# A decoder block on one core: the second group's first weights a step later, small loads behind x's tiles, x2's stores ahead of gate's rows

## The chip, the cores and the metric

The kernel runs on one core of one Trainium2 chip. The metric is device time in microseconds (us) of one execution, lower is better. The kernel before takes 1216.88 us, the median of three runs (1215.8 to 1218.68). All numbers of the profile come from one further execution, taken by the hardware profiler.

## What is computed

One layer for 1024 tokens of width 1024, all in float32. The reference, cut to what matters:

```python
h = rms_norm(x, norm1_g)
rq, rk, rv, rg, dq, dk, dv = split(h @ w_in)            # 512 columns each
# eight retention heads: rotary on q and k, chunks of 128 tokens with a running state
ret = rms_norm(retention(rotary(rq), rotary(rk) * 64 ** -0.5, rv), ret_norm_g) * silu(rg)
# four differential heads: two softmax maps each over normed q and k
q_d, k_d = rms_norm(dq, diff_q_norm_g), rms_norm(dk, diff_k_norm_g)
lam = exp(sum(lambda_q1 * lambda_k1)) - exp(sum(lambda_q2 * lambda_k2)) + LAMBDA_INIT
dif = (softmax(q1 k1^T / 8) - lam * softmax(q2 k2^T / 8)) @ dv
dif = rms_norm(dif, diff_subln_g) * (1 - LAMBDA_INIT)
x = x + concat([ret, dif]) @ w_out
h2 = rms_norm(x, norm2_g)
x = x + (silu(h2 @ w_gate) * (h2 @ w_up)) @ w_down      # 2816 hidden columns
```

## The kernel before

**Split products.** A float32 operand is held as two parts: `hi`, rounded by ScalarE (ACT), and `lo`, the rest, taken by VectorE (DVE). Each product is three matmuls on TensorE (PE): hi by hi, hi by lo, lo by hi. Weights come in rows of 128 (a tile `raw`), are scaled and split by `load_w` into `whi` and `wlo`, and stay in SBUF for a group. In the profile, a split of a weight is one ACT row `whi<-raw` and one DVE row `wlo<-raw`. There are two `raw` buffers, so a third row is not loaded before the first has been split.

**Steps.** Steps 0 to 31 are the four differential heads by eight token tiles. In step s the projection of head s // 8 and tile s % 8 (`proj`, 8 chunks of three matmuls, 384 wide, into a PSUM tile `pp`) is the spine; after each chunk k stand the pieces of other work that `DIF_PLAN` names as (lag, k, function). So the attention of a tile runs one to three steps behind its projection: `d_sq` and `d_qkn` norm q and k, `d_qkturn` turns them (PE, `m<-cs,qkn`), `d_qkhi`, `d_qlo`, `d_klo` split them into `q`, `kh`, `kl`, `d_scores` multiplies (`big<-kh,q`), `d_max`, `d_exp`, `d_weights` make the softmax. Beside this, x itself is turned in steps 0 to 5: `x_load(t)` brings tile t (SyncE's queue, tile `p`), `x_turn(t, half)` turns it (PE, `m<-cs,p`, four 128x128), `x_split(t, half)` splits the turned half (ACT `CAST act<-m`, then DVE `act<-m,act`). Tiles 0 to 3 are loaded at the start, tile t from 4 on in step t - 3, and turned in step t - 2. All turns share two PSUM buffers `m`: a turn waits until what was turned two turns back has been split.

**Weights of the next group.** The table `ready` gives each step the rows of weights that are loaded for it (`w_load(s + 1)`, at the beginning of step s) and split in it (`w_part(s)`, ACT behind chunk 5 and DVE behind chunk 6). Head 1's row k stands at step k: one row a step from step 0 on.

**Small loads.** `small_loads` at the end of step 0 issues ten little transfers: the gains `gq`, `gk` (two each), the four lambda vectors (`lam`) and the two output gains (`gout`). In step 1 `gains` scales gq and gout, and `lambdas` makes minus lambda (`nlam`): product and sum on DVE (`lprod`, `lsum`), `lexp` on ACT, two rows on DVE.

**After the heads.** Steps 32 to 63 are retention (512 wide), steps 64 to 66 the first three tiles of the output projection. `r_tables` makes retention's tables `rms`, `vdec`, `eps` on DVE from the means `ms`. Then `mid` runs the remaining 13 half tiles of the output projection, 8 chunks each, with `MID_PLAN` naming (chunk, function): `o_load` loads a half tile of x (`xr`), `o_add` adds it to the product and stores the sum to DRAM (`x2d<-x`), `n_square`, `n_rs`, `n_scale` norm it in place (so `n_scale` waits for the store), `n_turn` turns it (PE, `h<-cs,x`). Gate's first two blocks of weights (`rawp<-in_w_gate_dram`, 512 KB each) are asked for at chunks 40 and 56, up's at chunk 111. The rest, from about 594 us on, is the feed-forward: `Strassen` products of seven matmul groups, one pair of gate and up columns at a time, then w_down.

**What sets the order.** Every engine takes its instructions in order. While `order["pinned"]` is set, the instructions that go through the wrapper `Pinned` stand as written; all else is placed by a scheduler, as early as its data and buffers allow. Before the change the wrapper covers the four computing engines, not SyncE (SP), and `r_tables` is called with pinning off. SP's queue issues nearly all transfers, one after the other; an issue that has to wait holds those behind it. The wrapper's line 377 stands in the profile as the source of every computing instruction, so rows are told apart by tile names.

Of the kernel before, what the change touches and what calls it, by code (L numbers as in the profile page):

```python
# [16 lines left out]
P = 128  # L17
# [3 lines left out]
KC = D // P  # L21
# [31 lines left out]
def constants():  # L53
# [68 lines left out]
    (0, "mix_turn", 0),  # L122
    (0, "o_load", 0, 1),
    (0, "mix_turn", 1),
# [239 lines left out]
def block_kernel(ctx: ExitStack, tc: tile.TileContext, x, norm1_g, w_in, ret_norm_g, dq_g, dk_g,  # L364
# [16 lines left out]

    V, A, G, T = Pinned(nc.vector), Pinned(nc.scalar), Pinned(nc.gpsimd), Pinned(nc.tensor)

    const = ctx.enter_context(tc.tile_pool(name="const", bufs=1))
# [149 lines left out]
    def load_x(t):  # L534
        xt[t] = dp.tile([P, S], F32, tag="p", name="p", bufs=NP)
        nc.sync.dma_start(xt[t], x[0, t * P:(t + 1) * P, :])

# [77 lines left out]
    def small_loads():  # L615
        for g_sb, g_dr in ((gq, dq_g), (gk, dk_g)):
            for m in range(2):
                nc.sync.dma_start(g_sb[m * HD:(m + 1) * HD, :], g_dr[0].rearrange("(d o) -> d o", o=1))
        for i, l_dr in enumerate((lq1, lq2, lk1, lk2)):
            nc.sync.dma_start(lam4[:, i, :], l_dr[0].partition_broadcast(P))  # L620
        nc.sync.dma_start(gout[:, 0:4], ret_norm_g[0].rearrange("h d -> (h d)").rearrange("(k p) -> p k", p=P))
        nc.sync.dma_start(gout[:, 4:5], subln_g[0].rearrange("(d o) -> d o", o=1))
# [4 lines left out]
    def gains():  # L627
        V.tensor_scalar_mul(gq, gq, HD ** -0.5)
        V.tensor_scalar_mul(gout[:, 0:4], gout[:, 0:4], HD ** 0.5)
        V.tensor_scalar_mul(gout[:, 4:5], gout[:, 4:5], 1.0 - LAMBDA_INIT)  # L630

    def lambdas():
        lprod = dp.tile([P, 2, HD], F32, tag="sqo", name="lprod", bufs=1)
        V.tensor_tensor(out=lprod, in0=lam4[:, 0:2, :], in1=lam4[:, 2:4, :], op=ALU.mult)
        V.tensor_reduce(out=lsum, in_=lprod, axis=AX.X, op=ALU.add)
        A.activation(lexp, lsum, AF.Exp)
        V.tensor_tensor(out=nlam, in0=lexp[:, 1:2], in1=lexp[:, 0:1], op=ALU.subtract)
        V.tensor_scalar_add(nlam, nlam, -LAMBDA_INIT)
# [305 lines left out]
    def o_add(t, dh):  # L944
        x2[t][dh] = (rowa if dh else rowb).tile([P, 512], F32, tag="rowa" if dh else "rowb", name="x2")
        V.tensor_tensor(out=x2[t][dh], in0=prs.pop(("o", t, dh)), in1=prs.pop(("x", t, dh)), op=ALU.add)
        nc.sync.dma_start(x2d[t * P:(t + 1) * P, dh * 512:(dh + 1) * 512], x2[t][dh])

# [6 lines left out]
    for g in range(1, NG + 1):  # L955
        for k in range(KC):
            s = (g - 1) * NT + k
            if g == NDH + 1:
                s = max(s, (g - 1) * NT + 4 + k // 2)
            ready.setdefault(s, []).append((g, k, "wp" if g % 2 == 0 else "wd" if g < NDH else "wr"))  # L960
# [17 lines left out]
    for s in range(ND + NR + 3):  # L978
        if s == ND:
# [6 lines left out]
            for qbd in qbd_t:  # L986
                G.memset(qbd, 0.0)
            r_tables()
        if s == ND + 2:
            difps.close()  # L990
# [11 lines left out]
        elif s == 1:  # L1002
            ops += [(5, gains), (7, lambdas)]
            ops += [(at, f, 2, *args) for at, f, *args in LATE]
        ops += [(0, w_load, s + 1)] + [(k, w_part, s) for k in W_PLAN]
        t = s - ND - NR
# [128 lines left out]
    class Strassen:  # L1135
# [9 lines left out]
        def load(self, j):  # L1145
            r = ap.tile([P, 4, 2, P], F32, tag="rawp", name="rawp", bufs=3)
            nc.sync.dma_start(r.rearrange("p k i e -> p k (i e)"),
                              self.source[0, j * 512:(j + 1) * 512, self.f0 * P:(self.f0 + 2) * P].rearrange(
# [251 lines left out]
```

## Time and profile before

| | |
|---|---|
| time, median of 3 runs | 1216.88 us (1215.8 to 1218.68) |
| time of the profiled execution | 1216.8 us |
| its span from first to last instruction | 1215.0 us |
| PE busy | 1200.5 us (99%), 5968 matmuls |
| DVE, ACT, POOL busy | 835.5, 537.1, 556.1 us |
| mean granted PE clock | 0.998 |

The span is 1.8 us shorter than the time of the same execution. PE's busy time counts a matmul from its start to its modelled end; successive matmuls overlap, so what counts for the path is where a row says that PE stood idle and for whom. The granted clock is the share of full speed that PE was given in a stretch: a matmul takes longer while it is below 1.

### The profile page before, as it was taken

The page shows a single profiled execution, that of the slowest core. Times are in us where ns is not written, and L with a number is a line of the kernel's source. Part 1 is how long each engine was busy: PE and PEld are TensorE (multiplying, and loading weights), DVE is VectorE, ACT ScalarE, POOL GpSimd, SP SyncE. Part 2 cuts the span into 40 slices and gives each one's busy share as a digit, 9 for nine tenths or more (in the row PEclk, how much of TensorE's full clock was granted, in tenths as well). Part 3 has the DMA queues.
Part 4 walks back from the last instruction along what each step waited for, and adds up shares of the span by engine and source line. Part 5 has one row for each costly group of instructions (what it writes and reads, how often), then busy time and mean ns, then how long its engine had stood idle before and what let it go on. Part 6 is the DMA issues. An engine that isn't in the chain of part 4 may idle for free.

```text
span 1215.0 us, 17362 instructions
## 1 busy us (share of the span) xinstructions
PE 1200.5 (99%) x5968; PEld 1020.6 (84%) x5968; DVE 835.5 (69%) x1501; ACT 537.1 (44%) x1194; POOL 556.1 (46%) x709
## 2 busy tenths in 40 slices
PE   7999999999999999999999999999999999999998
PEld 6899989888888888788888888888888888888887
DVE  5988888864444445545989766766666659798697
ACT  5866666653322233433634344343443434444442
POOL 2655555545444434100056556544565436154053
PEclk9999999999999999999999999999999999999999
DMA  6201011103111111422133333323333168943342
GB/s 202 62 27 32 22 36 36 36 10 102 46 36 44 35 35 36 148 92 91 61 104 122 113 104 113 115 85 104 105 113 114 68 233 289 365 136 95 95 120 81
DMA packets 97383, 117.34 MB, mean 97 GB/s; under 512 B 8976, under 2 KB 60304, under 8 KB 97296
## 3 DMA queue, kind: packets, MB, share of 16 engines
q1 hardware_dynamic: 95968, 115.65, 29.5%
q8 instruction: 47, 0.77, 0.3%
q10 hardware_dynamic: 1328, 0.60, 0.2%
q14 instruction: 40, 0.33, 0.1%
HBM read 87.64 MB, written 28.57 MB: 96 GB/s over the span
## 4 chain that ended last, share of the span: by engine, by line
PE 94%; DVE 3%; DMA 1%; ACT 1%; issue 1%; POOL 0%; DVEq 0%; ACTq 0%; POOLq 0%
PE pp L377 43%; PE h L377 27%; PE m L377 19%; PE big L377 3%; PE o L377 2%; PE it L377 1%; DMA raw<-in_w_in_dram 1%; DVE act L377 1%; DMA x2d<-x 0%; DVE wlo L377 0%; DVE q L377 0%; DVE x L377 0%; DVE acc L377 0%; ACT kh L377 0%; DVE sum L377 0%
## 5 line engine op out<-in xcount | busy, mean ns | idle before, releaser
L377 PE MATMUL pp<-whi,act 128*128 128x384 f32 (+1 forms) x896 | 287.2, 373 | 0.8 <-ACT whi L377 0.8
L377 POOL TENSOR_TENSOR sum<-rawp 128x512 f32<-128x512 f32 x100 | 142.0, 1422 | 174.0 <-DVE wlo L377 172.3
L377 ACT CAST whi<-sum 128x512 fp32r<-128x512 f32 x165 | 102.6, 622 | 201.8 <-POOL sum L377 65.7
L377 DVE TENSOR_TENSOR wlo<-sum,whi 128x512 fp32r<-128x512 f32 x165 | 166.4, 1008 | 35.0 <-ACT whi L377 34.8
L377 PE MATMUL h<-act,whi 128*128 128x512 f32 x608 | 187.2, 389 | 0.0
L377 PEld LDWEIGHTS pp<-whi,act 128*128 128x128 f32 x896 | 167.2, 189 | 15.3 <-ACT whi L377 1.0
L377 PE MATMUL pp<-wlo,act 128*128 128x384 f32 (+1 forms) x448 | 161.6, 361 | 0.6 <-DVE wlo L377 0.6
L377 POOL TENSOR_TENSOR sum<-wide 128x512 f32<-128x512 f32 x55 | 86.9, 1581 | 127.4 <-DVE wlo L377 99.0
L377 PEld LDWEIGHTS h<-act,whi 128*128 128x128 f32 x608 | 114.1, 188 | 23.6
L377 PE MATMUL pp<-wrh,act 128*128 128x512 f32 x384 | 131.3, 402 | 0.0
L377 PE MATMUL h<-act,wlo 128*128 128x512 f32 x304 | 118.3, 389 | 0.0
L377 DVE TENSOR_TENSOR wlo<-wide,whi 128x512 fp32r<-128x512 f32 x99 | 79.2, 823 | 32.1 <-ACT whi L377 32.1
L377 PE MATMUL pp<-act,whi 128*128 128x512 f32 (+2 forms) x320 | 97.2, 385 | 0.2 <-DVE act L377 0.2
L377 PE MATMUL m<-act,whi 128*128 128x512 f32 (+2 forms) x320 | 97.0, 385 | 0.0
L377 ACT CAST whi<-wide 128x512 fp32r<-128x512 f32 x99 | 59.3, 621 | 83.4 <-PE m L377 43.2
L377 PEld LDWEIGHTS pp<-wlo,act 128*128 128x128 f32 x448 | 84.9, 190 | 7.7 <-DVE wlo L377 1.2
L377 PEld LDWEIGHTS pp<-wrh,act 128*128 128x128 f32 x384 | 72.2, 188 | 14.3
L377 POOL TENSOR_TENSOR fsum<-c 128x512 f32<-128x512 f32 x55 | 79.3, 1452 | 10.0 <-DMA ffd<-fsum 10.0
L377 DVE TENSOR_TENSOR c<-c,h 128x512 f32<-128x512 f32 x86 | 56.8, 682 | 30.0 <-PE h L377 30.0
L377 PE MATMUL pp<-wrl,act 128*128 128x512 f32 x192 | 74.8, 390 | 0.0
L377 DVE TENSOR_TENSOR wlo<-rawp,whi 128x512 fp32r<-128x512 f32 x44 | 47.8, 1087 | 38.7 <-ACT whi L377 37.9
L377 PEld LDWEIGHTS pp<-act,whi 128*128 128x128 f32 x320 | 59.8, 188 | 12.2 <-DVE act L377 0.4
(163 smaller groups left out, 2514.8 us busy)
## 6 DMA issues: line engine op xcount, KB each, us to landing
wide<-ffd SPq DMA_DIRECT2D x77, 256.0 KB, 2.8
ffd<-fsum SPq DMA_DIRECT2D x55, 256.0 KB, 2.0
rawp<-in_w_gate_dram SPq DMA_DIRECT2D x22, 512.0 KB, 3.8
rawp<-in_w_up_dram SPq DMA_DIRECT2D x22, 512.0 KB, 3.8
wide<-in_w_down_dram SPq DMA_DIRECT2D x44, 256.0 KB, 5.4
raw<-in_w_in_dram SPq DMA_DIRECT2D x32, 256.0 KB, 2.8
ffd<-c SPq DMA_DIRECT2D x22, 256.0 KB, 2.0
raw<-in_w_in_dram SPq DMA_DIRECT2D x26, 192.0 KB, 2.5
```

The costliest lines, as they stand in the source:

```text
L377: i = getattr(self.engine, op)(*args, **kw)
```

## The change

- Head 1's row 0 moves from step 0 to step 1, where row 1 already stands: two rows are split in step 1, none in step 0. In step 1 the loads for step 2 (`w_load`) stand behind the last chunk in place of the first.
- Of the ten small loads, `gq` and `gk` stay; the four of lambda and the two of `gout` become `late_loads` in step 1. The scaling of `gout` and lambda's product and sum move to step 2 (chunk 2), its exponential and the two rows behind it to chunk 6 of step 2.
- SP gets a wrapper of its own, `SY`, which is used for x's tiles, x2's stores and gate's and up's blocks: these now stand in program order among the pinned work.
- `r_tables` is pinned, so it stands where it is written, at step 32.
- The second of two equal loads `o_load(0, 1)` goes.

```diff
 MID_PLAN = [
     (0, "mix_turn", 0),
-    (0, "o_load", 0, 1),
     (0, "mix_turn", 1),
...
     V, A, G, T = Pinned(nc.vector), Pinned(nc.scalar), Pinned(nc.gpsimd), Pinned(nc.tensor)
+    SY = Pinned(nc.sync)
...
     def load_x(t):
         xt[t] = dp.tile([P, S], F32, tag="p", name="p", bufs=NP)
-        nc.sync.dma_start(xt[t], x[0, t * P:(t + 1) * P, :])
+        SY.dma_start(xt[t], x[0, t * P:(t + 1) * P, :])
...
                 nc.sync.dma_start(g_sb[m * HD:(m + 1) * HD, :], g_dr[0].rearrange("(d o) -> d o", o=1))
+
+    def late_loads():
         for i, l_dr in enumerate((lq1, lq2, lk1, lk2)):
             nc.sync.dma_start(lam4[:, i, :], l_dr[0].partition_broadcast(P))
         nc.sync.dma_start(gout[:, 0:4], ret_norm_g[0].rearrange("h d -> (h d)").rearrange("(k p) -> p k", p=P))
...
     def gains():
         V.tensor_scalar_mul(gq, gq, HD ** -0.5)
+
+    def late_gains():
         V.tensor_scalar_mul(gout[:, 0:4], gout[:, 0:4], HD ** 0.5)
         V.tensor_scalar_mul(gout[:, 4:5], gout[:, 4:5], 1.0 - LAMBDA_INIT)
 
     def lambdas():
+        late_gains()
         lprod = dp.tile([P, 2, HD], F32, tag="sqo", name="lprod", bufs=1)
         V.tensor_tensor(out=lprod, in0=lam4[:, 0:2, :], in1=lam4[:, 2:4, :], op=ALU.mult)
         V.tensor_reduce(out=lsum, in_=lprod, axis=AX.X, op=ALU.add)
+
+    def minus_lambda():
         A.activation(lexp, lsum, AF.Exp)
...
         V.tensor_tensor(out=x2[t][dh], in0=prs.pop(("o", t, dh)), in1=prs.pop(("x", t, dh)), op=ALU.add)
-        nc.sync.dma_start(x2d[t * P:(t + 1) * P, dh * 512:(dh + 1) * 512], x2[t][dh])
+        SY.dma_start(x2d[t * P:(t + 1) * P, dh * 512:(dh + 1) * 512], x2[t][dh])
...
             s = (g - 1) * NT + k
+            if g == 1:
+
+                s = max(s, 1)
             if g == NDH + 1:
...
+            order["pinned"] = True
             r_tables()
+            order["pinned"] = False
...
         elif s == 1:
-            ops += [(5, gains), (7, lambdas)]
+            ops += [(3, late_loads), (5, gains)]
             ops += [(at, f, 2, *args) for at, f, *args in LATE]
-        ops += [(0, w_load, s + 1)] + [(k, w_part, s) for k in W_PLAN]
+        elif s == 2:
+            ops += [(2, lambdas), (6, minus_lambda)]
+        ops += [(KC - 1 if s == 1 else 0, w_load, s + 1)] + [(k, w_part, s) for k in W_PLAN]
...
             r = ap.tile([P, 4, 2, P], F32, tag="rawp", name="rawp", bufs=3)
-            nc.sync.dma_start(r.rearrange("p k i e -> p k (i e)"),
+            SY.dma_start(r.rearrange("p k i e -> p k (i e)"),
```

PE's and POOL's instructions stand in the same order before and after. Three places on the other engines follow. First, DVE in steps 1 and 2, from the scaling of `gq` on. Before (`act<-m,act` is the `lo` part of a half of x, `ss`, `qkn` the norm of q and k, `big`, `nm` the scores' mask and maximum):

```order
L377 TENSOR_SCALAR gq<-gq 128x1
L377 TENSOR_SCALAR gout<-gout 128x4
L377 TENSOR_SCALAR gout<-gout 128x1
L377 SCALAR_TENSOR_TENSOR wlo<-raw,g1col,whi 128x384
L377 SCALAR_TENSOR_TENSOR q<-m,gq,q 64x128 x2
L377 SCALAR_TENSOR_TENSOR kl<-m,gk,kh 128x128
L377 CAST kh<-kh 64x128 x2
L377 TENSOR_TENSOR lprod<-lam_182 128x128
L377 TENSOR_REDUCE lsum<-lprod 128x2
L377 TENSOR_TENSOR nlam<-lexp 128x1
L377 TENSOR_SCALAR nlam<-nlam 128x1
```

After:

```order
L376 TENSOR_SCALAR gq<-gq 128x1
L376 SCALAR_TENSOR_TENSOR wlo<-raw,g1col,whi 128x384 x2
L376 SCALAR_TENSOR_TENSOR q<-m,gq,q 64x128 x2
L376 SCALAR_TENSOR_TENSOR kl<-m,gk,kh 128x128
L376 CAST kh<-kh 64x128 x2
L376 TENSOR_REDUCE ss_375<-sq 128x4
L376 TENSOR_TENSOR act<-m,act 128x512
L376 TENSOR_SCALAR gout<-gout 128x4
L376 TENSOR_SCALAR gout<-gout 128x1
L376 TENSOR_TENSOR lprod<-lam_182 128x128
L376 TENSOR_REDUCE lsum<-lprod 128x2
```

Two splits stand together behind `gq`, and the norm's sum `ss` stands directly behind `kh`; the rows of `gout` and lambda come behind the next `act`, and the two `nlam` rows six rows further on, directly ahead of the next `wlo`.

Second, SP's queue in the first steps (`raw` are rows of head 1's weights, `p` tiles of x). Before:

```order
L441 DMA raw<-in_w_in_dram 128x3x128 x2
L618 DMA gq<-in_diff_q_norm_g_dram 64x1 x2
L618 DMA gk<-in_diff_k_norm_g_dram 64x1 x2
L620 DMA lam_182<-in_lambda_q_dram 128x64 x2
L620 DMA lam_182<-in_lambda_k_dram 128x64 x2
L621 DMA gout<-in_ret_norm_g_dram 128x4x1
L622 DMA gout<-in_diff_subln_g_dram 128x1
L441 DMA raw<-in_w_in_dram 128x3x128
L536 DMA p<-in_x_dram 128x1024 x2
L441 DMA raw<-in_w_in_dram 128x3x128 x2
```

After:

```order
L441 DMA raw<-in_w_in_dram 128x3x128 x2
L618 DMA gq<-in_diff_q_norm_g_dram 64x1 x2
L618 DMA gk<-in_diff_k_norm_g_dram 64x1 x2
L376 DMA p<-in_x_dram 128x1024
L622 DMA lam_182<-in_lambda_q_dram 128x64 x2
L622 DMA lam_182<-in_lambda_k_dram 128x64 x2
L623 DMA gout<-in_ret_norm_g_dram 128x4x1
L624 DMA gout<-in_diff_subln_g_dram 128x1
L441 DMA raw<-in_w_in_dram 128x3x128 x2
L376 DMA p<-in_x_dram 128x1024
L441 DMA raw<-in_w_in_dram 128x3x128
```

Tile 4 of x moves ahead of the six small loads; tile 5 moves behind two rows of weights.

Third, SP's queue around the beginning of `mid`. Before:

```order
L947 DMA x2d<-x_6277 128x512
L939 DMA xr<-in_x_dram 128x512 x2
L1147 DMA rawp<-in_w_gate_dram 128x4x256
L947 DMA x2d<-x_6331 128x512
L939 DMA xr<-in_x_dram 128x512
L1147 DMA rawp<-in_w_gate_dram 128x4x256
L947 DMA x2d<-x_6408 128x512
L939 DMA xr<-in_x_dram 128x512
```

After:

```order
L376 DMA x2d<-x_6277 128x512
L946 DMA xr<-in_x_dram 128x512
L376 DMA x2d<-x_6331 128x512
L946 DMA xr<-in_x_dram 128x512
L376 DMA x2d<-x_6406 128x512
L946 DMA xr<-in_x_dram 128x512
L376 DMA x2d<-x_6462 128x512
```

Gate's two blocks go from among the stores of the second to fourth half tile to behind those of the seventh and ninth, and one `xr` is gone.

## The prediction

> **What bounds the kernel now.** I read the page first, then the windows, PE's timeline, and for each gap the rows of the engine it waits for.
>
> ```profile
> PE 1200.5 (99%) x5968; PEld 1020.6 (84%) x5968; DVE 835.5 (69%) x1501; ACT 537.1 (44%) x1194; POOL 556.1 (46%) x709
> 28.00:43.00 15.00, 13.77 (x85) 11.94 (x84) 13.55 (x39) 11.89 (x34) 9.14 (x21) 1.00 0.26 64
> 250.00:500.00 250.00, 250.00 (x1315) 212.44 (x1314) 119.63 (x322) 84.40 (x236) 107.45 (x197) 1.00 0.15 46
> 500.00:515.00 15.00, 13.82 (x70) 11.25 (x69) 7.00 (x11) 6.46 (x15) 1.44 (x5) 1.00 0.65 212
> ```
>
> PE bounds the whole: 1200.5 of 1215.0 us. The windows (stretch, length, then busy time of PE, PEld, DVE, ACT and POOL, granted clock, DMA) say where it does not: 1.2 us stand open in both 28 to 43 and 500 to 515, nothing from 250 to 500. The change moves no matmul, so it can only take idle time from PE or make its clock better. PE's timeline shows where (start, duration; in brackets the idle time before and for whom):
>
> ```profile
> 15.16 0.60 PE L377 MATMUL m<-cs,p 128*128 128x128 f32 x4
> 18.89 1.11 PE L377 MATMUL m<-cs,p 128*128 128x128 f32 x4 [1.69 <-DVE act L377]
> 30.72 0.41 PE L377 MATMUL m<-cs,qkn 128*128 128x128 f32 x2 [0.70 <-DVE qkn L377]
> 67.21 0.41 PE L377 MATMUL m<-cs,qkn 128*128 128x128 f32 x2 [0.60 <-DVE vdec L377]
> 513.47 0.66 PE L377 MATMUL h<-cs,x 128*128 128x128 f32 x4 [1.18 <-DVE x L377]
> ```
>
> Four gaps: 1.69 us in step 1, 0.70 in step 2, 0.60 at 67, 1.18 at 513. Behind the first the clock falls (windows, columns as above):
>
> ```profile
> 16.00:19.00 3.00, 1.05 (x7) 0.53 (x6) 1.87 (x4) 2.03 (x5) 0.46 (x2) 0.98 0.17 31
> 19.00:22.00 3.00, 3.00 (x12) 2.90 (x13) 1.83 (x4) 1.71 (x4) 1.51 (x3) 0.50 0.40 64
> 22.00:23.00 1.00, 1.00 (x8) 1.00 (x7) 0.00 (x0) 0.35 (x1) 0.77 (x2) 0.85 1.12 421
> ```
>
> If the clock is either full or half, as 0.50 suggests, 0.98 and 0.85 say that PE ran at half of it from about 18.9 to 22.3 us.
>
> **The first gap.** Its chain, on the chain of waits (first row), ACT and DVE:
>
> ```profile
> 8.95 8.00 DMA raw<-in_w_in_dram
> 16.97 0.61 ACT L377 ACTIVATE whi<-raw,g1col 128x384 fp32r<-128x384 f32 x1 [1.21 <-DMA raw<-in_w_in_dram]
> 17.49 0.57 ACT L377 CAST act<-m 128x512 fp32r<-128x512 f32 x1
> 15.80 0.69 DVE L377 TENSOR_TENSOR act<-m,act 128x512 fp32r<-128x512 f32 x1 [1.09 <-ACT act L377]
> 17.62 0.62 DVE L377 SCALAR_TENSOR_TENSOR wlo<-raw,g1col,whi 128x384 fp32r<-128x384 f32 x1 [1.13 <-ACT whi L377]
> 18.16 0.68 DVE L377 TENSOR_TENSOR act<-m,act 128x512 fp32r<-128x512 f32 x1
> ```
>
> The row for head 1 lands at 16.95. ACT waits 1.21 us for it, DVE 1.13 behind ACT, and both queues hold x's next half behind that: it was turned by 15.76 (15.16 + 0.60) and is rounded only at 17.49. The change takes this split out of step 0. ACT's `CAST` then follows the turn at 15.8, DVE's `act` starts at about 16.4 (behind its row of 15.80) and ends at 17.1, and PE's turn of 18.89 can start at 17.15: 1.74 us earlier, without a gap.
>
> With no gap I take the clock as full: the 3.4 us at half of it hold 1.7 us of work, so another 1.7 go. PE would be 3.4 us early at 22.3, if the other engines follow.
>
> [...]
>
> **Steps 1 and 2, now on DVE's time.** Window 28 to 43 has DVE busy for 13.55 of 15 us: what PE wins is kept only as far as DVE comes along.
>
> ```profile
> 27.60 0.20 ACT L377 ACTIVATE lexp<-lsum 128x2 f32<-128x2 f32 x1 [2.32 <-DVE lsum L377]
> 25.32 0.72 DVE L377 SCALAR_TENSOR_TENSOR q<-m,gq,q 64x128 fp32r<-64x128 f32 x2 [0.64 <-ACT kh L377]
> 26.45 0.47 DVE L377 CAST kh<-kh 64x128 fp32r<-64x128 f32 x2
> 28.11 0.42 DVE L377 TENSOR_REDUCE ss<-sq 128x4 f32<-128x256 f32 x1
> 30.15 0.42 DVE L377 TENSOR_TENSOR qkn<-pp,rs 128x256 f32<-128x256 f32 x1
> 31.62 0.61 DVE L377 SCALAR_TENSOR_TENSOR wlo<-raw,g1col,whi 128x384 fp32r<-128x384 f32 x1
> 33.37 0.47 DVE L377 CAST kh<-kh 64x128 fp32r<-64x128 f32 x2
> 33.74 0.35 PE L377 MATMUL big<-kh,q 128*128 128x256 f32 x1
> ```
>
> ACT stands 2.32 us at `lexp`, so the next norm's square and DVE's `ss` come late, and 0.70 of PE's idle time hangs on that. Worked out in the new order, with all that PE sends 3.4 us earlier: DVE, done with one split at 24.7 (25.32 less 0.64), would be done at 21.3, and with the second, 0.62, at 21.9; ACT's `kh`, for which `q` waited, also comes 3.4 earlier, at 21.9. So `q` stands at 22.0 in place of 25.32. The rows to the end of `kh` keep their 1.6 us (to 23.6), and `ss` follows there in place of 28.11, 4.5 earlier, since lambda is gone from between (26.92 to 28.11 before). Between `ss` and `qkn` (2.04 us before, set by POOL's norm) come two rows of `gout` and two of lambda, 0.85 by the 0.2 to 0.3 of such small rows; POOL's norm hides some 0.4 of it, so `qkn` stands near 26.1 in place of 30.15. PE's turn behind it comes at 26.6, then ACT's `q`, `kh` and `lexp`, some 0.4 apart, end at 28.0; DVE, ready 1.47 behind `qkn` (31.62 less 30.15) at 27.6, waits for `lexp`, makes the two `nlam` rows (0.35) and starts `wlo` at 28.35 in place of 31.62. From there on DVE's order is as before, and PE's scores wait for `kh` (33.74 is just behind 33.37): PE, less than 3.0 behind its turn of 26.6 (33.74 less 30.72), gets there near 29.4, finds `kh` near 30.3 and stands about 1 us, a new gap in step 3. **The front is worth 3.3 us**, what DVE gives. Its bounds: 4.1 if `lexp` costs DVE nothing (30.15 to 26.1), 1.7 if only the first gap goes and neither the clock nor lambda's wait.
>
> Two loads must be in time for that. The landings of tiles `p` in the first 60 us, SP's row of lambda and PE's turns of tiles 4 and 5:
>
> ```profile
> DMA to landing us min/median/max: 3.5/4.4/7.6
> 15.38 1.37 SPq L620 DMA_DIRECT2D lam<-in_lambda_q_dram  x2
> 25.83 0.60 PE L377 MATMUL m<-cs,p 128*128 128x128 f32 x4
> 32.56 0.60 PE L377 MATMUL m<-cs,p 128*128 128x128 f32 x4
> ```
>
> Tile 4 takes lambda's place at 15.4 and lands at 19.8 (23.0 at worst); its turn (25.83) now comes at 22.4. Tile 5 stands behind two weight rows that wait for the two splits, so it is issued near 22.5 and lands at 26.9 (30.1 at worst); its turn (32.56, 1.84 behind 30.72) comes at 28.4, and up to 29.5 a delay is hidden by the wait for `kh`. The six small loads are needed from 24.6 on; they follow tile 4 by a few us.
>
> **The gap at 67.** `rms` waits for the last mean and holds the queue:
>
> ```profile
> 65.71 0.20 DVE L377 RECIPROCAL rms<-ms 128x8 f32<-128x8 f32 x1 [1.75 <-POOL ms L377]
> 64.35 1.04 POOL L377 TENSOR_TENSOR rs<-ms,cs 128x4 f32<-128x4 f32 x1
> ```
>
> Pinned to step 32, it leaves: the maximum behind it starts near 64.0, 1.75 earlier, `qkn` when POOL's `rs` ends (65.4), PE's turn has its operand at 65.9 in place of 67.2. The 0.60 go. In step 32 the three rows cost DVE some 0.6 us; there PE is never idle (from 250 to 500 us), and DVE is under half busy. If that cover failed it would cost the 0.6 again.
>
> **The gap at 513.** `n_scale` works in place and waits for the store of its half tile:
>
> ```profile
> 502.13 0.38 SPq L1147 DMA_DIRECT2D rawp<-in_w_gate_dram  x1
> 507.83 4.74 DMA x2d<-x
> 509.70 0.75 DVE L377 SCALAR_TENSOR_TENSOR x<-x,sso,gtile 128x512 f32<-128x512 f32 x1 [1.90 <-POOL sso L377]
> 512.67 0.75 DVE L377 SCALAR_TENSOR_TENSOR x<-x,sso,gtile 128x512 f32<-128x512 f32 x1 [2.22 <-DMA x2d<-x]
> x2d<-x SPq DMA_DIRECT2D x16, 256.0 KB, 2.0
> 569.07 0.68 DVE L377 TENSOR_TENSOR sum<-rawp 128x512 f32<-128x512 f32 x1
> ```
>
> The first of gate's two blocks of 512 KB goes out at 502.13, the second behind the next store; both stand ahead of a store that takes 4.74 us where the median of sixteen is 2.0. With gate's blocks gone from there and one 256 KB load less, it lands at 509.9, DVE goes straight from the first `n_scale` to the second (ends 511.2), and PE, ready at 512.3 (513.47 less 1.18), does not wait. Even a store of 3.5 us would do. Gate's blocks now go out behind chunks 40 and 56, some 30 us later, and DVE reads them from chunk 89 on (569.07): at 0.75 us a chunk (67 us over 89), 25 us behind the second, several times what any 512 KB above took. The store of the seventh half tile stands ahead of the first block, so no later store is caught.
>
> **Sum.** 3.3 + 0.60 + 1.18 = 5.1 us. The profiled execution takes 1216.8 (span 1215.0 and 1.8 around it), the median is 1216.88, so the two can be taken as one: **1211.8 us**, between 1.7 (the front's lower bound, nothing else) and 5.9 (its upper, and the other two) below 1216.9, so 1211.0 to 1215.2. A difference under 0.2% (2.4 us) is about what a measurement of this kernel can't tell from none.
>
> **Rivals.**
>
> A. *The wait moves to step 3.* The new gap of 1.2 us grows: ACT's queue has one weight split more ahead of `lexp` (0.6), or tile 5 takes its longest 7.6 us (0.6 past the cover). Speaks for it: DVE's 13.55 of 15. Front 2.1, total 3.9: 1213.0.
>
> B. *The half clock does not come from that gap and falls all the same.* PE is 1.7 us less early through steps 1 and 2, and ACT's `kh` and so DVE's `q` come 1.6 later than above. Front 1.7, total 3.5: 1213.4. Against it: the gap stands directly ahead of the fall. For it: the gap of 1.18 at 513 brought none (window 500 to 515, clock 1.00). [...]
>
> C. *No change that can be told.* DVE bounds from step 1 on, and the work that the change puts there (one split, 0.6; lambda's wait and rows, 0.9) eats the 1.74. Front 0.2, total 2.0: 1214.9. Against it: DVE still stands idle before `q` (0.64).
>
> D. *Slower.* Tile 5 is late by a whole split: its place in SP's row is held by head 1's next row, whose split comes at 28.35 to 28.95, and with the longest landing it is there at 36.5. PE, in order, stands at its turn until then: 7.0 us past 29.5, and a half clock behind such a gap (1.7). 5.1 less 8.7: 1220.5. It decides from a landing at 32.9 on (29.5 + 5.1 - 1.7), slower by 0.2% from 35.3. Against it: both `raw` buffers are free near 21.9, and the longest landing is 7.6.
>
> **Chances.** Forecast 0.55, A 0.15, B 0.10, C 0.13, D 0.07. Faster by over 0.2% are the forecast, A and B and a little of C: 0.81; within 0.2% the most of C, 0.13; slower D, 0.06. The range, 1209.8 to 1214.5, takes in A and B; below, it allows that a gap counts more than its idle time, since a matmul's end overlaps the next one's start, and some 1 us between measurements.
>
> **What would show it.** Right: PE's turn of x near 17.2 without a gap and the clock at 1.00 from 16 to 24; `ss` on DVE near 23.7; PE waiting about 1 us for `kh` near 29 to 30; `rms` gone from 65 and no gap at 67; the store near 507 landing in about 2 us and no gap behind it; the later span as long as before. Wrong: a half clock still at 19 or new at 29, PE waiting for a DMA of `p` in step 2 or 3, or DVE's rows at 43 less than 3 us early.

## The result

The changed kernel takes 1210.39 us (median of six runs, 1209.99 to 1211.38) against 1216.34 us for the kernel before beside it (six runs, 1215.2 to 1218.95): a ratio of 0.9949, with a 95% interval of 0.9936 to 0.9962. Measured once more, with other runs of the kernel before, it took 1210.57 against 1215.94, a ratio of 0.9954 (0.9942 to 0.9967). It is 5.4 to 6.0 us faster by the medians. The profiled execution of the changed kernel took 1210.4 us with a span of 1208.6, which is 6.4 us less than the span of before.

The page and the windows of the changed kernel, columns as in the prediction:

```profile
PE 1199.0 (99%) x5968; PEld 1020.0 (84%) x5968; DVE 834.1 (69%) x1501; ACT 537.6 (44%) x1194; POOL 556.6 (46%) x709
16.00:19.00 3.00, 3.00 (x21) 2.75 (x22) 2.49 (x5) 2.66 (x7) 1.32 (x2) 1.00 0.67 202
19.00:22.00 3.00, 3.00 (x20) 2.93 (x19) 2.35 (x6) 2.79 (x7) 1.54 (x5) 1.00 0.31 45
28.00:43.00 15.00, 13.62 (x85) 12.01 (x84) 13.57 (x37) 11.11 (x33) 8.71 (x20) 1.00 0.32 98
500.00:515.00 15.00, 15.00 (x76) 12.49 (x75) 7.29 (x11) 5.39 (x13) 1.74 (x5) 1.00 0.32 110
```

PE is busy without a break from 16 to 22 us and from 500 to 515, and the half clock at 19 is gone (1.00). From 28 to 43 about as much stays open as before (13.62 busy, 13.77 then). The timelines of PE and DVE of the changed kernel at the places that the prediction names:

```profile
15.98 1.27 PE L376 MATMUL m<-cs,p 128*128 128x128 f32 x8 [0.26 <-DVE act L376]
29.83 0.36 PE L376 MATMUL big<-kh,q 128*128 128x256 f32 x1 [0.90 <-DVE kh L376]
62.39 0.34 PE L376 MATMUL pp<-whi,act 128*128 128x384 f32 x1
62.57 0.38 PE L376 MATMUL m<-cs,qkn 128*128 128x128 f32 x2
506.02 0.60 PE L376 MATMUL h<-cs,x 128*128 128x128 f32 x4
507.15 0.60 PE L376 MATMUL h<-cs,x 128*128 128x128 f32 x4
15.23 1.31 DVE L376 TENSOR_TENSOR act<-m,act 128x512 fp32r<-128x512 f32 x2 [1.09 <-ACT act L376]
23.08 0.42 DVE L376 TENSOR_REDUCE ss<-sq 128x4 f32<-128x256 f32 x1
25.19 0.41 DVE L376 TENSOR_TENSOR qkn<-pp,rs 128x256 f32<-128x256 f32 x1
27.38 0.23 DVE L376 TENSOR_TENSOR nlam<-lexp 128x1 f32<-128x1 f32 x1 [0.64 <-ACT lexp L376]
27.71 0.61 DVE L376 SCALAR_TENSOR_TENSOR wlo<-raw,g1col,whi 128x384 fp32r<-128x384 f32 x1
```

The two turns that a gap of 1.69 us divided are one row of eight now. PE's waits for `qkn` and `vdec` are gone, the one for `kh` has come. At 507 the second turn stands 1.13 us behind the first.

**Where the 6.4 us are.** Four rows of before complete the comparison (timelines of PE):

```profile
11.63 0.63 PE L377 MATMUL m<-cs,p 128*128 128x128 f32 x4 [1.14 <-DMA p<-in_x_dram]
62.38 0.39 PE L377 MATMUL big<-kh,q 128*128 128x512 f32 x1
68.59 0.42 PE L377 MATMUL pp<-whi,act 128*128 128x384 f32 x1
511.00 0.60 PE L377 MATMUL h<-cs,x 128*128 128x128 f32 x4
```

and their counterparts in the changed kernel:

```profile
11.05 0.63 PE L376 MATMUL m<-cs,p 128*128 128x128 f32 x4
58.48 0.39 PE L376 MATMUL big<-kh,q 128*128 128x512 f32 x1
63.82 0.42 PE L376 MATMUL pp<-whi,act 128*128 128x384 f32 x1
```

| place | row before, row after | ahead, us | this piece, us |
|---|---|---|---|
| start, nothing changed yet | `act` 15.80, 15.23 | 0.57 | 0.57 |
| front, to step 3's split | `wlo` 31.62, 27.71 | 3.91 | 3.34 |
| up to the gap at 67 | `big` 62.38, 58.48 | 3.90 | 0 |
| gap at 67 | `pp` 68.59, 63.82 | 4.77 | 0.87 |
| up to the turn at 511 | `h` 511.00, 506.02 | 4.98 | 0.2 |
| gap at 513 | `h` 513.47, 507.15 | 6.32 | 1.34 |
| end | span 1215.0, 1208.6 | 6.4 | 0.1 |

The forecast's terms were 3.3, 0.60 and 1.18. The 0.57 at the start come before any instruction that the change moves: in the profile of before PE waits 1.14 us for a tile of x there, in this one it doesn't. From 515 us on nothing differs: PE is busy for 664.79 us between 515 and 1180 in both.

### The profile page after: what moved, and what is told of

It reads as the page before. It is cut to its first block, busy times and chain, and to the rows that moved or that the text cites. A ratio compares the mean times of both kernels' runs of the same rounds, so it can differ in the third digit from the quotient of the medians.

```text
span 1208.6 us, 17360 instructions
## 1 busy us (share of the span) xinstructions
PE 1199.0 (99%) x5968; PEld 1020.0 (84%) x5968; DVE 834.1 (69%) x1501; ACT 537.6 (44%) x1194; POOL 556.6 (46%) x709
## 4 chain that ended last, share of the span: by engine, by line
PE 96%; DVE 2%; ACT 1%; DMA 0%; issue 0%; SPq 0%; ACTq 0%; DVEq 0%
PE pp L376 44%; PE h L376 27%; PE m L376 19%; PE big L376 3%; PE o L376 2%; PE it L376 1%; DVE act L376 0%; DMA more<-in_w_in_dram 0%; DVE q L376 0%; DVE acc L376 0%; ACT kh L376 0%; DVE wlo L376 0%; DVE kl L376 0%; DVE sum L376 0%; DVE kh L376 0%
## 5 line engine op out<-in xcount | busy, mean ns | idle before, releaser
L376 PEld LDWEIGHTS h<-act,whi 128*128 128x128 f32 x608 | 114.0, 188 | 23.6
L376 PEld LDWEIGHTS pp<-wrh,act 128*128 128x128 f32 x384 | 72.2, 188 | 14.3
```

The lines of the kernel that those rows point to most:

```text
L376: i = getattr(self.engine, op)(*args, **kw)
```

## Experiments: the front in its parts

The total agrees, so the question is whether the terms do. The front's theory has three links: the first gap, the half clock behind it (the stretch with a granted clock of 0.50), and lambda's wait. Each run below is compared with runs of the kernel before on the same chip. To leave out the chance at the start, the profiles are compared by one distance: from DVE's `act` (15.80 in before, with its wait of 1.09 for ACT, no row ahead of it changed) to the split `wlo` at the start of step 3 (31.62): 15.82 us before, 12.48 after.

**The front's edits alone.** The diff of the change without its edits to `o_add`, the class's `load`, `r_tables` and the double load.

> The kernel before with the front's edits alone: head 1's row 0 a step later, the loads for step 2 behind step 1's last chunk, x's tiles in program order, the six small loads and lambda a step later. The tables, x2's stores, gate's rows and the double load stay as before. Forecast's theory: the front is worth 3.3 us (the rows of steps 1 to 3 as in the changed kernel, `ss` near 23.7, no half clock, a wait of about 1 us for `kh`), and the gaps of 0.60 at 67 and 1.18 at 513 stay, each about 3.3 us earlier. Rival, half clock not from that gap: 1.7 us. Rival, chance at the start: the changed kernel's profile is 0.57 us ahead of the kernel before at 15 us, where nothing has been changed yet; if that is the edits' work it is here too, in a way that all profiles show (total 3.9); if it is chance, the profiles differ in it among themselves.

Measured: 1214.13 against 1215.81 us, ratio 0.9986 (0.9978 to 0.9995), so 1.7 us faster, 0.6 to 2.7. The rows are the changed kernel's (timeline of DVE):

```profile
14.84 1.33 DVE L377 TENSOR_TENSOR act<-m,act 128x512 fp32r<-128x512 f32 x2 [1.09 <-ACT act L377]
27.35 0.61 DVE L377 SCALAR_TENSOR_TENSOR wlo<-raw,g1col,whi 128x384 fp32r<-128x384 f32 x1
```

The distance is 12.51, so 3.3 us less than in the profile of before, and yet the times differ by half of that. The two can only agree if the profile of before shows more than its usual execution has.

**The weights' part alone**, lambda and the six small loads where they were:

```diff
+            if g == 1:
+                s = max(s, 1)
...
-        ops += [(0, w_load, s + 1)] + [(k, w_part, s) for k in W_PLAN]
+        ops += [(KC - 1 if s == 1 else 0, w_load, s + 1)] + [(k, w_part, s) for k in W_PLAN]
```

> The kernel before with head 1's row 0 a step later (and the loads for step 2 behind step 1's last chunk, x's tiles in program order), but the six small loads and lambda where they were: in steps 0 and 1. Forecast's theory: the first gap and the half clock go, PE is 3.4 us early at 22; `lexp` and the two `nlam` rows stand ahead of `ss`, which comes near 24.8 in place of 23.6, and `wlo`, 1.47 behind `qkn`, near 28.3: worth 3.0 to 3.3 us, so that lambda's move alone is worth at most 0.3. Rival, lambda's wait takes the place: ACT's 2.32 us wait at `lexp` stays and holds DVE's norm; front 1.7 to 2.3 us, so that lambda's move is worth 1.0 to 1.6. Rival, half clock not from that gap: 0.50 still in the granted clock near 19 to 22.

Measured: 1215.6 against 1215.81, ratio 0.9997 (0.9986 to 1.0008): nothing that the times show, between 1.7 us faster and 1.0 slower. My theory's 3.0 to 3.3 is wrong here, and the rival's 1.7 to 2.3 lies at the edge of the interval at best (timelines of ACT, DVE and PE of this run):

```profile
25.93 0.20 ACT L377 ACTIVATE lexp<-lsum 128x2 f32<-128x2 f32 x1 [3.28 <-DVE lsum L377]
22.09 0.32 DVE L377 TENSOR_SCALAR gout<-gout 128x4 f32<-128x4 f32 x2 [0.65 <-DMA gout<-in_ret_norm_g_dram]
29.05 0.41 PE L377 MATMUL m<-cs,qkn 128*128 128x128 f32 x2 [0.71 <-DVE qkn L377]
```

With PE early, ACT waits 3.28 us for lambda's sum in place of 2.32, DVE waits 0.65 for one of the small loads that now is too late, and PE's wait for `qkn` is back. The distance is 14.41.

DVE's `q` tells which of these holds the front. From `q` to `wlo` DVE takes 6.30 us here (23.65 to 29.95), 6.30 before (25.32 to 31.62) and 6.27 in the changed kernel (21.44 to 27.71): it makes no difference there where lambda's rows stand, and the rival's mechanism, lambda's wait, is not what costs. From `act` to `q` DVE takes 8.11 us here and 6.21 in the changed kernel. So the 1.9 us lie ahead of `q`, where DVE stands for `gout`, a load that was issued at 17.68 and for which DVE waits until 22.09. My theory had left that load out. This is read from rows; no run moves `gout` alone.

**Lambda's part alone**, head 1's row 0 still in step 0:

```diff
-            ops += [(5, gains), (7, lambdas)]
+            ops += [(3, late_loads), (5, gains)]
...
+        elif s == 2:
+            ops += [(2, lambdas), (6, minus_lambda)]
```

> The kernel before with the six small loads and lambda a step later alone (x's tiles in program order too); head 1's row 0 stays in step 0. Forecast's theory: the first gap (1.69 us for `act`) and the half clock behind it stay, since ACT still waits for head 1's row; the 0.70 us gap at `qkn` near 30.7 goes, at most 0.7 us faster. Rival, lambda's wait is what bounds steps 1 and 2: 1.0 to 1.6 us faster with the first gap in place.

Measured: 1216.55 against 1215.81, ratio 1.0007 (0.9998 to 1.0015): nothing. The first gap stays, as expected; the half clock behind it does not. The timeline of PE:

```profile
18.34 0.66 PE L377 MATMUL m<-cs,p 128*128 128x128 f32 x4 [1.83 <-DVE act L377]
512.75 1.11 PE L377 MATMUL h<-cs,x 128*128 128x128 f32 x4 [2.50 <-DVE x L377]
```

and the windows of this run:

```profile
17.31:20.73 3.42, 2.40 (x17) 2.36 (x18) 2.96 (x6) 2.91 (x8) 1.32 (x2) 1.00 0.58 159
20.73:24.14 3.41, 3.41 (x24) 3.35 (x23) 2.19 (x6) 2.30 (x6) 1.54 (x5) 1.00 0.49 117
512.24:515.65 3.41, 2.90 (x9) 2.51 (x10) 2.19 (x4) 0.94 (x2) 0.00 (x0) 0.50 0.00 0
```

A gap of 1.83 us, longer than the 1.69 of before, and the clock is full behind it. At 512 the same execution has a half clock, behind a wait of 2.50. The distance is 14.32.

**The gap filled.** The kernel before, with one matmul more where PE waits:

```diff
+FILL = 1
...
+    def filler():
+        fill = dps.tile([P, S], F32, tag="big", name="fill")
+        for i in range(FILL):
+            T.matmul(fill[:, :512], ident, xt[3][:, :512], start=True, stop=True)
...
-            ops += [(5, gains), (7, lambdas)]
+            ops += [(1, filler), (5, gains), (7, lambdas)]
```

> The kernel before with one more matmul (x's half tile by the identity, 512 wide, float32, into a PSUM tile that nothing reads) between the two turns of x around the first gap. It takes PE about as long as the gap (the two of the same kind at the start take 3.78 us), so PE waits little for `act`, and the turn behind it still comes near 18.9. Forecast's theory, the gap brings the half clock: the granted clock stays at 1.00 from 19 to 22.3, PE reaches the turn of 21.72 some 1.4 us and the work at 22.3 some 1.7 us earlier, and what DVE and ACT follow of that, 0.5 to 1.7 us, is won. Rival, the half clock comes from something else (a fixed time after the start, or the mix of work): 0.50 from 19 to 22 all the same, time as before or up to 0.3 us more.

Measured: 1215.54 against 1215.81, ratio 1.0003 (0.9994 to 1.0012): nothing. In the profile the clock is full. The timeline of PE:

```profile
17.16 1.02 PE L378 MATMUL fill<-p,cs 128*128 128x512 f32 x2
19.02 0.66 PE L378 MATMUL m<-cs,p 128*128 128x128 f32 x4 [0.84 <-DVE act L378]
```

and the windows of this run:

```profile
19.00:22.00 3.00, 2.98 (x20) 2.95 (x21) 2.09 (x5) 2.49 (x6) 1.80 (x4) 1.00 0.37 55
```

The distance is 14.25, 1.57 less than in the profile of before. The old front without a filler and without the half clock has 14.49 (table below), 1.33 less. So the half clock cost 1.3 to 1.6 us in that one execution. But the times say that a full clock at this place is nothing unusual. So the half clock is a thing of some executions, and the profile of before caught one.

The distances of all these side by side, with two profiles of kernels that have the old front (they are described further on):

| kernel | `act` to `wlo` | first gap | half clock behind it |
|---|---|---|---|
| before | 15.82 | 1.69 | yes |
| old front, stores moved | 15.81 | 1.69 | yes |
| old front, one load less | 14.49 | 1.80 | no |
| gap filled | 14.25 | 0.84 | no |
| lambda's part alone | 14.32 | 1.83 | no |
| weights' part alone | 14.41 | none | no (one ahead of `act`, at 9.36) |
| front's edits alone | 12.51 | none | no |
| changed kernel, twice | 12.48, 12.48 | none | no |

Without the half clock the old front takes 14.5 us, and either part alone leaves it at 14.3 to 14.4. Both together make it 12.5, that is 2.0 less, which agrees with the measured 1.7.

The stretch from `act` to `q` shows why neither part gains alone. It is 8.18 us in the old front without the half clock (one load less), 8.08 with lambda's part alone, 8.11 with the weights' part alone, and 6.25 and 6.21 with both (front's edits alone, changed kernel). Two things stand ahead of `q` on DVE: the split that waits for head 1's row, and the scaling that waits for `gout`. While one of them is left, `q` comes as late as with both.

## Experiments: when the clock falls

**A ladder of gaps.** The changed kernel with a stall made on purpose in 26 steps of retention, where PE otherwise never waits (busy for 250.00 of 250 us from 250 to 500 in the changed kernel); the copies are work that the reference has no use for:

```diff
+    GAPS = {s: (2, 4, 5, 6, 8)[s % 5] for s in range(36, 62)}
+
+    def gap(n):
+        lad = rp.tile([P, 256], F32, name="lad", bufs=1)
+        one = bankm([P, 256])
+        T.matmul(one, ident, cs[:, :256], start=True, stop=True)
+        V.tensor_copy(lad, one)
+        for _ in range(n - 1):
+            V.tensor_copy(lad, lad)
+        two = bankm([P, 256])
+        T.matmul(two, ident, lad, start=True, stop=True)
...
+        if s in GAPS:
+            ops += [(4, gap, GAPS[s])]
```

> The changed kernel with a stall made on purpose in each of steps 36 to 61, in a stretch where PE otherwise never waits: a short matmul, then 2, 4, 5, 6 or 8 copies on DVE, one after the other, then a matmul that reads the last copy, so that PE stands for some 1 to 4 us. Theory, a window of 3.4 us that runs freely: the half clock follows only those stalls that leave one such window mostly idle, so stalls of one length bring it at some places and not at others, those near 1.7 us seldom, those over 3 us mostly or always; the half clocks last 3.4 us each and begin a whole number of 3.4 us apart. Rival, a length decides: all stalls over some length bring it, none below. [...]

Measured, one execution: PE stands 0.94, 1.59, 1.92, 2.25 or 2.90 us, the same at each place with the same number of copies. A half clock follows none of the five stalls of 0.94, none of the six of 1.59, one of five of 1.92, one of five of 2.25, and all five of 2.90. The half clocks begin at 313.88, 365.08, 395.80, 416.28, 470.90, 511.86 and 522.10 us. Between them lie 15, 9, 6, 16, 12 and 3 times 3.413 us, to within 0.02. So the half clocks of this run begin on one grid of 3.413 us, over 61 windows of it. The profile of before shows such a grid over its whole length: the clock falls at 18.89 and once more at 1213.56, when PE has finished (windows of before: 1.00 up to 1213.55, 0.57 from there to 1213.60, then 0.50), 350 times 3.4133 us later. By the rows that follow, what goes with a half clock is how busy PE was in the window ahead of it (windows of this run on that grid, in pairs: the one that holds the most of a stall, and the next):

```profile
310.47:313.88 3.41, 1.22 (x6) 1.06 (x7) 1.84 (x7) 0.00 (x0) 0.00 (x0) 1.00 0.00 0
313.88:317.30 3.42, 3.42 (x14) 3.03 (x13) 1.61 (x3) 1.07 (x4) 1.23 (x2) 0.50 0.00 0
392.39:395.80 3.41, 1.49 (x8) 1.23 (x8) 1.60 (x5) 0.00 (x0) 0.21 (x1) 1.00 0.00 0
395.80:399.22 3.42, 3.42 (x14) 2.94 (x14) 0.95 (x2) 1.07 (x4) 1.35 (x2) 0.50 0.00 0
498.20:501.61 3.41, 1.49 (x10) 1.34 (x9) 1.60 (x5) 0.00 (x0) 0.00 (x0) 1.00 0.00 0
501.61:505.02 3.41, 3.41 (x20) 2.89 (x20) 1.90 (x5) 1.15 (x5) 1.70 (x3) 1.00 0.08 16
```

With 1.22 us busy of 3.41 the next window runs at half clock; with 1.49 it does at 395.80 and doesn't at 501.61, so in this run the border lies near 1.5. The first gap of before, cut into windows of the same length (windows of before):

```profile
15.48:18.89 3.41, 1.47 (x10) 0.91 (x8) 1.96 (x4) 2.20 (x6) 0.89 (x3) 1.00 0.32 70
18.89:22.30 3.41, 3.41 (x13) 3.31 (x14) 1.94 (x4) 1.82 (x4) 1.78 (x4) 0.50 0.46 93
```

1.47 us: just under the border. The gap of 1.69 and the one of 0.26 ahead of it lie from 16.28 to 18.89, 2.61 us long; a window must hold nearly all of that to come under the border, and of the 3.41 us over which its start can fall, 0.80 do that: one execution in four, an estimate. That the start falls differently from execution to execution the rows show: a window begins 3.09 us behind `act` in before (18.89 and 15.80), 3.77 with the stores moved (19.93 and 16.16) and 2.21 with lambda's part alone (17.31, counted back from its half clock at 512.24, and 15.10). In the four profiles with this gap it came twice, which is too few to tell one in four from one in two; the 1.7 us that the front gained alone, where 2.0 are to be had without any half clock, speaks for seldom. So do the eleven runs of the kernel with the old front and the stores moved: eight lie between 1213.07 and 1214.19 us, three between 1214.82 and 1215.92, the profiled one with its half clock the longest. This is no proof, since the start alone varies by over 1 us (`act` between 14.78 and 16.22).

Two of the other three profiles agree. With the stores moved, the window ahead of the half clock (16.52 to 19.93) holds 1.45 us. With lambda's part alone, the window from 508.83 to 512.24 holds 1.42, and the next runs at half; counted back by 144 windows (an estimate from the 3.4133 us of before), the one from 17.31 to 20.73 holds 2.40, and the clock stays full behind it. With one load less the clock is 1.00 from 16 to 22; where a window begins in that execution no row shows, so it says nothing for or against.

## Experiments: the stores, the double load and the tables

**The stores put back.** The changed kernel with x2's stores and gate's and up's blocks free for the scheduler again, the double load still gone:

```diff
-        SY.dma_start(x2d[t * P:(t + 1) * P, dh * 512:(dh + 1) * 512], x2[t][dh])
+        nc.sync.dma_start(x2d[t * P:(t + 1) * P, dh * 512:(dh + 1) * 512], x2[t][dh])
...
-            SY.dma_start(r.rearrange("p k i e -> p k (i e)"),
+            nc.sync.dma_start(r.rearrange("p k i e -> p k (i e)"),
```

> The changed kernel with x2's stores and gate's blocks back in the scheduler's order, so that gate's two blocks stand among the stores of the second to fourth half tile again; the double load stays gone. Forecast's theory: the wait of 1.18 us at `h<-cs,x` near 507 comes back, 1.2 to 1.4 us slower than the changed kernel's 1210.4 (1211.7), less if the double load was what held the store. Theory after the front's runs, in which the store took 5.3 to 6.1 us and the wait was 1.0 to 2.5 us: the profile of the kernel before had a short one, and this term is 1.2 to 2.7 us, with a half clock of 3.4 us behind it in some executions (1.7 more): a median near 1212.6, and a wider spread than the changed kernel's 1.4 us. Rival, the double load alone held the store: as the changed kernel.

Measured: 1212.2 us, ratio 0.9962 (0.9949 to 0.9974) to the kernel before, so 1.6 to 1.8 slower than the changed kernel by the medians, between the two theories' 1211.7 and 1212.6. By the ratios it is 1.0 to 1.6, and their intervals overlap; the spread of 1.2 us is not the wider one that the second theory expected. The wait is back (timeline of PE):

```profile
508.04 0.66 PE L376 MATMUL h<-cs,x 128*128 128x128 f32 x4 [1.09 <-DVE x L376]
```

**The stores' part alone**: the kernel before with x2's stores and the blocks in program order (the two lines above the other way round) and the double load gone.

> The kernel before with x2's stores and gate's and up's blocks in program order and the double load gone, nothing else. Forecast's theory: 1.18 us, the wait that the profile of before shows at 513. Theory after the first runs: with two blocks and the double load ahead of it the store takes 4.7 to 6.1 us and PE's wait is 1.0 to 2.5 us, in five profiles 1.7 on the average, and matmuls that no longer overlap add some 0.2: worth 1.9 us, and more where a half clock follows; a median near 1214.0 beside 1216.0 for before. Rival, the three edits are worth more together than alone (the whole change gained 6, the front alone 1.7, and undoing the stores and the tables cost 1.6 and 1.2): 3 us or more here.

Measured: 1213.52 against 1215.94 us, ratio 0.9982 (0.9973 to 0.9991): 2.2 us faster, 1.1 to 3.3, near the second theory's 1.9 and nearly twice the forecast's 1.18, which still lies just inside the interval. PE doesn't wait at 511 there (windows of this run; the second shows the half clock at the front, which this kernel keeps):

```profile
500.00:515.00 15.00, 15.00 (x76) 12.47 (x75) 7.86 (x12) 7.30 (x17) 1.83 (x6) 1.00 0.41 138
19.93:23.34 3.41, 3.41 (x14) 3.31 (x14) 1.39 (x4) 2.40 (x5) 2.06 (x5) 0.50 0.78 221
```

**The double load alone**:

```diff
 MID_PLAN = [
     (0, "mix_turn", 0),
-    (0, "o_load", 0, 1),
```

> The kernel before without the second of the two equal loads, nothing else: 256 KB less ahead of the third half tile's store, gate's two blocks still there. Forecast's theory (one load of 256 KB beside two blocks of 512): a small part of the wait at 513, 0.2 to 0.6 us. Rival, the blocks alone hold the store: no difference. Rival, the double load is the one that matters, since it is issued last ahead of the first block: 1 us or more, the wait at 513 gone.

Measured: 1216.08 against 1215.94, ratio 1.0001 (0.9992 to 1.001): nothing, and the wait is there (timeline of PE):

```profile
511.53 0.66 PE L376 MATMUL h<-cs,x 128*128 128x128 f32 x4 [1.42 <-DVE x L376]
```

So gate's two blocks hold the store, which took 4.74 us behind them in before. In the seven profiles that have them there, this wait of PE is 1.18 (before), 1.75, 2.01, 2.50, 1.03, 1.09 and 1.42 us, on the average 1.6; the one of before is among the short ones. With the blocks gone the stores land in 2.1 us (transfers of the changed kernel from 495 to 515):

```profile
x2d<-x SPq DMA_DIRECT2D x3, 256.0 KB, 2.1
```

**The tables put back**, the changed kernel with `r_tables` called with pinning off:

```diff
-            order["pinned"] = True
             r_tables()
-            order["pinned"] = False
```

> The changed kernel with retention's tables back where the scheduler puts them, with `rms` ahead of the tenth step's maximum. Forecast's theory: the wait of 0.60 us at `vdec` comes back near 62, 0.6 us slower than the changed kernel's 1210.4; by the two profiles, where the rows around the wait moved from 3.90 to 4.77 us ahead, 0.9 us slower. Rival, DVE's rows in step 32 cost as much as they did at 67: no difference.

Measured: 1211.74 us, ratio 0.9959 (0.9945 to 0.9973), 1.2 to 1.4 us slower than the changed kernel by the medians and 0.6 to 1.2 by the ratios. The intervals of the ratios overlap, so the times tell it neither from 0.6 or 0.9 nor surely from none. The profile does: PE's wait is back with its old length (timeline of PE):

```profile
63.67 0.41 PE L376 MATMUL m<-cs,qkn 128*128 128x128 f32 x2 [0.61 <-DVE vdec L376]
```

## Experiments: the new wait, and the start

**Lambda's rows earlier.** In the changed kernel DVE waits 0.64 for `lexp` ahead of `wlo`, and PE 0.90 for `kh` behind that.

```diff
-            ops += [(2, lambdas), (6, minus_lambda)]
+            ops += [(2, lambdas), (3, minus_lambda)]
```

> The changed kernel with lambda's exponential and its two rows at chunk 3 of step 2 in place of chunk 6: `lexp` goes ahead of ACT's next `CAST`, the two `nlam` rows ahead of `qkn`. If the wait of 0.64 us for `lexp`, ahead of `wlo`, is what holds DVE, and so PE's 0.90 us wait for `kh` near 29.8, it gains up to 0.6 us on the changed kernel (1209.8). Rival: the two rows and the wait for `lexp` now stand ahead of `qkn`, PE's turn of it comes some 0.4 us later, and nothing is gained or up to 0.4 us lost.

Measured: 1209.32 us, ratio 0.9941 (0.9928 to 0.9953). The distance from `act` to `wlo` falls from 12.48 to 11.73, and PE no longer waits for `kh` (timelines of DVE and PE; PE's row has no wait in it):

```profile
16.22 1.33 DVE L376 TENSOR_TENSOR act<-m,act 128x512 fp32r<-128x512 f32 x2 [1.09 <-ACT act L376]
26.22 0.17 DVE L376 TENSOR_TENSOR nlam<-lexp 128x1 f32<-128x1 f32 x1
27.95 0.61 DVE L376 SCALAR_TENSOR_TENSOR wlo<-raw,g1col,whi 128x384 fp32r<-128x384 f32 x1
30.07 0.36 PE L376 MATMUL big<-kh,q 128*128 128x256 f32 x1
```

That is 1.1 us better than the changed kernel, but measured beside other runs. So both once more on one chip:

> The changed kernel itself, beside the next one on the same chip: 1210.4 us. Its start, up to PE's second turn of x after the first group's weights, hangs on when the first tiles of x and the first weights land; if the 0.57 us that its first profile was ahead there were chance, this profile stands elsewhere, within the 15.6 to 17.0 us at which that turn stood in the other profiles of kernels that are alike up to there.

> The changed kernel with lambda's exponential and its two rows at chunk 3 of step 2, again, now beside the changed kernel on the same chip. By the first time (1209.3 beside 1210.4 measured apart) and by its profile (no wait of 0.90 us for `kh` near 30): 0.7 to 1.0 us faster than the changed kernel. Rival, the first difference was one of the start: none.

Measured: 1210.57 us, ratio 0.9954 (0.9942 to 0.9967), for the changed kernel and 1210.64, ratio 0.9950 (0.9938 to 0.9963), with lambda's rows earlier. The times don't tell the two apart. In the second profile with lambda's rows earlier the distance from `act` to `wlo` is 12.50, no shorter than the changed kernel's: this execution has a half clock from 9.01 to 12.42, ahead of `act`, which put PE 0.8 us later beside that row. From PE's first product behind the two turns (17.00 in the changed kernel, 18.02 and 17.96 with lambda's rows earlier) to the `big` row (29.83, 30.07, 30.01) it is 12.83 us in the changed kernel and 12.05 in both others. That it is the better kernel by 0.7 to 0.8 us is argued from these rows, not shown by times. The second profile of the changed kernel has its `act` at 14.90, the first at 15.23; over all profiles, all alike up to there, it stands between 14.78 and 16.22. The 0.57 us at the start were chance.

## Why the prediction was right, and where only its sum was

The forecast was 1211.8 us, 5.1 us less than before; measured are 1210.4 to 1210.6, 5.4 to 6.0 less. The direction and the places hold. The time lies below 1211.0, the lower end of the sum's own bounds, though inside the range; part of that is that the kernel before took 1215.9 to 1216.3 beside it, not 1216.88. The front's term was too large and the one at 513 probably too small, so that the sum came out as near as it did by some luck.

- **The first gap: right.** PE's turn was to come at 17.15 without a gap; it comes at 16.6 (the second half of the row at 15.98, 1.27 long), 17.2 with the 0.57 of the start added.
- **The half clock: right for the one execution, wrong for the median.** The step that failed is "With no gap I take the clock as full ... so another 1.7 go". The half clock did follow the gap, behind a window with 1.47 us busy, and it cost 1.3 to 1.6 there. But by the estimate above it does so in one of four executions, as the windows happen to lie, and the times are medians. Rival B had a half clock that falls whether the gap is there or not; no profile without the gap has one at that place, and the ladder, with a half clock behind all five stalls of 2.90 us and behind none of the five of 0.94, speaks against it too. That its number for the front, 1.7, is what was measured is chance.
- **DVE's rows in steps 1 and 2: right to 0.1 us, `qkn` to 0.35.** With 0.57 added for the start, `ss` stands at 23.65 (forecast 23.6), `qkn` at 25.76 (26.1), `nlam` at 27.95 (28.0), `wlo` at 28.28 (28.35), and PE waits 0.90 us for `kh` (about 1; rival A calls the same gap 1.2). What the forecast didn't name is why the small loads have to move: not for lambda's place in the order, which is worth nothing from `q` to `wlo`, but because DVE, once early, stands for `gout`. The front's 3.3 is 3.34 in the pair of profiles, and 1.7 (0.6 to 2.7) in the times.
- **The tables: right by the rows.** 0.60 forecast, 0.87 between the profiles, since the wait breaks a stream in which matmuls overlap: 66.27 to 67.21 between starts before (0.34 long and 0.60 idle), 62.39 to 62.57 after, 0.76 of difference. That DVE's work in step 32 costs nothing holds too: PE is busy for 250.00 of 250 us there.
- **The gap at 513: mechanism right, size probably too small.** 1.18 was read from a profile with a short wait; it is 1.03 to 2.50 in seven profiles, 1.6 on the average, and the part is worth 2.2 us (1.1 to 3.3, so 1.18 is not ruled out by the times). With the wait of 2.50 the clock fell to 0.50 besides. The double load, which the forecast counted among the causes, has no share that can be measured.
- **Rivals.** A (the wait moves to step 3) and C (no change) didn't happen: the new wait is 0.90 and not more. D (tile 5 late) neither: PE waits for no tile of x in steps 2 and 3.

By parts, 1.7 for the front, 2.2 for the stores and 0.6 to 1.2 for the tables make 4.5 to 5.1, and the whole 5.6 (4.0 to 7.1) to 6.2 (4.6 to 7.8). The intervals are too wide to say whether the parts make up the whole. The forecast's 5.1 was 3.3, 0.6 and 1.18: 1.3 to 1.6 of the front's term belonged to the half clock of one execution, and about 1.0 was missing at 513.

## What to carry to other kernels

A stall that a profile shows is one draw (the wait at 513 was 1.03 to 2.50 us in seven profiles, and the half clock followed the first gap in two of four): before a term rests on a transfer's landing or on a half clock, see how the same place looks in other profiles, or count the term with the chance that it comes. Where two waits hang on one engine's queue, taking one away can be worth nothing until the other goes too: here DVE waited for a row of weights and for a small load ahead of the same instruction, each half of the front's edits gained nothing that could be measured, and both gained 1.7 us. Keep large loads that nobody needs yet from going out ahead of a small store that someone waits for: x2's store took 4.74 us behind gate's two blocks of 512 KB in before, and 2.1 without them in the changed kernel.

## What the hardware showed unexpectedly

- The seven half clocks of the ladder begin on one grid of 3.413 us, and the two falls of the clock in before lie 350 such windows apart (18.89 and 1213.56). Behind the windows with 1.22 and 1.41 us busy (ladder), 1.42 (lambda's part alone), 1.45 (stores moved) and 1.47 (before) the next ran at half; behind three with 1.49 (ladder) it did once, at 395.80, and stayed full at 406.04 and 501.61; behind one with 2.40 (lambda's part alone) it stayed full.
- Behind a window that was itself at half clock the border lay higher: with 2.50 us busy the next one was at half clock too, with 2.90 (the window from 512.24 above) it was full. The first is from the ladder's run:

```profile
416.28:419.69 3.41, 2.50 (x7) 2.08 (x8) 0.69 (x3) 0.00 (x0) 0.00 (x0) 0.50 0.00 0
419.69:423.10 3.41, 3.41 (x13) 3.02 (x13) 0.95 (x2) 1.07 (x4) 1.34 (x2) 0.50 0.02 5
```

- At the start of an execution a half clock followed a busier window too, of 2.03 us (windows of the run with the weights' part alone); what else than busy time counts there stays open:

```profile
5.95:9.36 3.41, 2.03 (x11) 1.21 (x9) 2.50 (x5) 3.12 (x7) 0.00 (x0) 1.00 1.16 314
9.36:12.77 3.41, 3.41 (x13) 3.31 (x14) 2.13 (x5) 1.79 (x4) 0.00 (x0) 0.50 1.08 368
```
